# The first projection of an encoder trunk: loads three blocks ahead, c spread by matmuls, u made by ScalarE, VectorE's order skewed

## The chip, the cores and the metric

The kernel runs on one core of one Trainium2 chip. The metric is the device time of one execution in microseconds (us), the median of several runs. The engines are named as in the profile: PE is TensorE's matmul, PEld its weight load, DVE VectorE, ACT ScalarE, POOL GpSimd, SP the engine that here issues all transfers.

## The reference

Two layers of an encoder on a sequence of 512 frames with 1024 channels. Only the start of layer 0 matters here: the modulation by the conditioning vector c, and the projection of the modulated input.

```
c_act = silu(c)                                        # (1, 1024)
mods  = split(c_act @ w_ada[i] + b_ada[i], 6)          # shift, scale, gate, twice
sh1, sc1, g1, sh2, sc2, g2 = mods
u     = x * (1.0 + sc1) + sh1                          # (512, 1024)
# layer 0, mixer A (gated linear attention):
q, k, v, g, gk_lr = split(u @ w_in, ...)               # widths 512, 512, 1024, 1024, 16
log_a = log_sigmoid(gk_lr @ w_gk2 + b_gk) / 16
...                                                    # chunks of 64, then out projection
x     = layer_norm(alpha * x + (1.0 + g1) * y)         # then the squared-ReLU MLP
```

## The kernel before

Activations lie transposed, channels on the 128 partitions and frames along the row: x is eight tiles `xs[k]` of 128x512. A product of float32 accuracy is made of three matmuls on rounded parts: each operand is split into a rounded part (`hi`, type fp32r) and a rest (`lo`), and hi*hi, hi*lo and lo*hi are added up in PSUM. For a weight block, `whi` is a copy of `raw` by ACT and `wlo = raw - whi` a subtraction by DVE. For u, ACT makes `u[k][:, 0]` (the hi part, `ar` in the trace) as `xs[k] * scale + shift`; the value without rounding is `uf`, and `ar <- uf, ar` is the subtraction that gives the lo part.

The first projection makes q and k: 1024 output channels in eight PSUM banks `pss[0..7]`, each over all 512 frames. Its loop runs over eight blocks k of 128 input channels, because u for block k can be made as soon as the shift and the scale of these 128 channels are known. They come from two blocks of `w_ada`, stored transposed (`ada`, 128x1024): DVE multiplies such a block by `csil`, the silu of c spread over all partitions, and sums along the row (`SCALAR_TENSOR_TENSOR raw<-raw,csil`, accumulated into a column of `mods`). A small addition (`mods<-mods,col`) adds the bias. So block k needs two `ada` blocks (512 KB each), `xs[k]` (256 KB) and a weight block `w_qk[k]` (512 KB), and ends in 24 matmuls: eight hi*hi, eight hi*lo, eight lo*hi.

Each compute engine runs its instructions in the order in which they were written (class `InOrder`; this is why nearly every line of the profile is L47). SP issues the transfers in order too; a transfer waits at SP until the buffer that it writes is free. All `ada` and weight blocks share one pool of five buffers (`rawp`, tag "raw"), so that in the first projection a block takes three of the five. A second pool, `act`, has 26 buffers of 128x1024 for activations. The weight splits `whi` and `wlo` have four buffers each.

The list `plan` holds every weight and `ada` block in the order of use; `emit_unit` takes the next one, issues its transfer and writes its split. `fill` calls it until `state["look"]` blocks are ready. After the projection the eight banks are evacuated into `qk` (`af` in the trace), sixteen matmuls make the low-rank gate (`gk_w`), and two passes over `w_v` (`vpass`) follow, between whose blocks the gate is computed head by head (`prep`). The matmuls of `prep` need `gk_sb`, the evacuated gate.

Of the kernel before, what the change touches and what calls it, by code (L numbers as in the profile page):

```python
# [59 lines left out]
def trunk(ctx, tc, xT, c, ada, cols, gk1, gk2, w_qk, w_v, w_g, w_go, a_qk, a_v, a_tab,  # L60
# [22 lines left out]
    def act_r():  # L83
        return act.tile([P, 2, S], F32R, tag="act", name=nm("ar"))
# [4 lines left out]
    def tt(eng, o, a, b, op):  # L89
        eng.tensor_tensor(out=o, in0=a, in1=b, op=op)  # L90
# [4 lines left out]
    def lo_of(eng, o, x, hi):  # L95
        return eng.tensor_tensor(out=o, in0=x, in1=hi.bitcast(F32), op=ALU.subtract)
# [11 lines left out]
    nc.sync.dma_start(out=csil, in_=c.to_broadcast([P, D]))  # L108
# [3 lines left out]
    for _ in range(5):  # L112
        T.matmul(warm, one[:, 0:P], one, start=True, stop=True)
    A.activation(out=csil, in_=csil, func=AF.Silu)
# [12 lines left out]
    def ada_unit(l, t, k):  # L127
        raw = rawp.tile([P, D], F32, tag="raw", name=nm("raw"))
        nc.sync.dma_start(out=raw, in_=ada[l, t * 8 + k])
        if (l, t, k) == (0, SH1, 0):  # L130
            nc.sync.dma_start(out=col, in_=cols)
            for ll in range(2):
                for ty in (SC1, G1, SC2, G2):
                    b = C_ADA + ll * 48 + ty * 8
                    G.tensor_scalar(out=col[:, b:b + 8], in0=col[:, b:b + 8], scalar1=1.0, scalar2=None, op0=ALU.add)
            G.tensor_scalar(out=bq8, in0=col[:, C_BQ:C_BQ + 8], scalar1=0.125, scalar2=None, op0=ALU.mult)
            G.tensor_scalar(out=nbgk, in0=col[:, C_BGK:C_BGK + 4], scalar1=-1.0, scalar2=None, op0=ALU.mult)
            G.tensor_scalar(out=gn2, in0=col[:, C_GN:C_GN + 8], scalar1=-0.5, scalar2=None, op0=ALU.mult)
        if t == SC1 and l == 0:
            nc.sync.dma_start(out=xs[k], in_=xT[k * P:(k + 1) * P, :])  # L140
        i = t * 8 + k
        V.scalar_tensor_tensor(out=raw, in0=raw, scalar=1.0, in1=csil, op0=ALU.mult, op1=ALU.mult,
                               accum_out=mods[:, l, i:i + 1])
        if l == 0 and t in (SH1, SC1):
            if t == SC1:
                m2 = mods[:, 0, 0:16].rearrange("p (a b) -> p a b", b=8)[:, :, k:k + 1]
                c2 = col[:, C_ADA:C_ADA + 16].rearrange("p (a b) -> p a b", b=8)[:, :, k:k + 1]
                tt(V, m2, m2, c2, ALU.add)
        elif t == G2:
            tt(V, mods[:, l, i:i + 1], mods[:, l, i:i + 1], col[:, C_ADA + l * 48 + i:C_ADA + l * 48 + i + 1], ALU.add)  # L150
        elif k == KT - 1:
            m8 = mods[:, l, t * 8:t * 8 + 8]
            tt(V, m8, m8, col[:, C_ADA + l * 48 + t * 8:C_ADA + l * 48 + t * 8 + 8], ALU.add)

# [14 lines left out]
    def emit_unit():  # L169
# [23 lines left out]
        if state["pos"] == 3:  # L193
            for q in range(2):
                nc.sync.dma_start(out=raw[:, q * S:(q + 1) * S], in_=what[:, q * S:(q + 1) * S])
        else:
            nc.sync.dma_start(out=raw, in_=what)
        hi, lo = split_w(kind in "fF")
        if state["pos"] == 3:
            V.tensor_copy(hi[:, 0:S], raw[:, 0:S])  # L200
            later.append(lambda: A.copy(out=hi[:, S:D], in_=raw[:, S:D]))
            later.append(lambda: lo_of(V, lo, raw, hi))
            ready_w.append((hi, lo))
            return
        if kind == "s":
            for q in range(2):
                A.copy(out=hi[:, q * S:(q + 1) * S], in_=raw[:, q * S:(q + 1) * S])
        else:
            A.copy(out=hi, in_=raw)
# [48 lines left out]
    for k in range(KT):  # L258
        plan.append(("a", (0, SH1, k)))
        plan.append(("a", (0, SC1, k)))  # L260
        plan.append(("s", w_qk[k]))
# [360 lines left out]
    def gla():  # L622
# [9 lines left out]

        u = [act_r() for _ in range(KT)]
        pss = [bank() for _ in range(8)]
        gk_t = wp.tile([P, D], F32R, tag="whi", name="gk_w")
# [5 lines left out]
        G.memset(eps_rms, RMS_EPS)  # L641
        for k in range(KT):
            emit_unit()
            emit_unit()
            if k == 0:
                emit_unit()
            A.activation(out=u[k][:, 0, :], in_=xs[k], func=AF.Identity, scale=mod(0, SC1, k), bias=mod(0, SH1, k))
            uf = gt.tile([P, S], F32, tag="t1", name=nm("uf"))
            V.tensor_scalar(out=uf, in0=xs[k], scalar1=mod(0, SC1, k), scalar2=mod(0, SH1, k), op0=ALU.mult, op1=ALU.add)
            w = next_w()  # L650
            lo_of(V, u[k][:, 1, :], uf, u[k][:, 0, :])
            for m in range(8):
                T.matmul(pss[m], wk(w, m)[0], uk(u, k)[0], start=(k == 0), stop=False)
# [25 lines left out]
        state["look"] = 3  # L679
        qk = [act_f() for _ in range(4)]  # L680
        for h in range(4):
            A.activation(out=qk[h][:, 0, :], in_=pss[h], func=AF.Copy, scale=float(P) ** -0.5)
            A.copy(out=qk[h][:, 1, :], in_=pss[4 + h])
# [547 lines left out]
```

## Time and profile before

| | |
|---|---|
| median of 3 runs | 1232.88 us (1232.21 to 1233.76) |
| the profiled execution | 1231.73 us, its span 1229.5 us |
| PE busy | 1181.4 us (96%), 5834 matmuls |
| PEld busy | 986.9 us (80%) |
| DVE busy | 834.3 us (68%) |
| ACT busy | 542.9 us (44%) |
| POOL busy | 185.4 us (15%) |
| first projection, first weight load to the next stage's first | 10.96 to 61.34 us |

The busy shares are means over the whole span. Matmuls are pipelined, so that PE is counted as busy while one is still draining; the weight loads, one ahead of each matmul, show the pace better. The time outside the span (2.2 us) belongs to the start and the end of the execution.

### The profile page before, as it was taken

What the parts mean: (1) busy time and instruction counts of PE and PEld (TensorE: products, weight loads), DVE (VectorE), ACT (ScalarE), POOL (GpSimd) and SP (SyncE); (2) the same over time, 40 slices, a digit from 0 to 9 for tenths busy, and PEclk for the clock granted to TensorE, in tenths of its full rate; (3) what the DMA queues carried; (4) which work ended last, traced back from release to release, by engine and by line L of the source; (5) the groups of instructions that cost most, each with busy time, mean ns of one, the idle gap of its engine ahead of it and who ended that gap; (6) DMA issues with size and microseconds to landing.
All of it is one profiled execution on the core that took longest, in us unless ns stands there. A gap on an engine that the chain in (4) does not pass through costs nothing.

```text
span 1229.5 us, 15417 instructions
## 1 busy us (share of the span) xinstructions
PE 1181.4 (96%) x5834; PEld 986.9 (80%) x5834; DVE 834.3 (68%) x1269; ACT 542.9 (44%) x864; POOL 185.4 (15%) x195
## 2 busy tenths in 40 slices
PE   8999999899999999999999999898999999999995
PEld 5678887788888888888888877668888888888885
DVE  6779579787667676667864788889865443443467
ACT  3265566365243243343483565573642322322324
POOL 2000001620000000004631132226200000000035
PEclk9999999999999999999999999999999999999998
DMA  8846634118878888764025431322165332232201
GB/s 310 280 155 209 230 110 140 50 41 282 284 268 316 280 291 310 261 250 154 2 78 180 146 135 71 128 87 69 35 204 156 92 106 93 88 107 97 89 15 69
DMA packets 57274, 192.68 MB, mean 157 GB/s; under 512 B 6448, under 2 KB 10800, under 8 KB 57200
## 3 DMA queue, kind: packets, MB, share of 16 engines
q1 hardware_dynamic: 57200, 191.70, 45.7%
q8 instruction: 46, 0.75, 0.3%
q14 instruction: 28, 0.23, 0.1%
HBM read 172.80 MB, written 18.87 MB: 156 GB/s over the span
## 4 chain that ended last, share of the span: by engine, by line
PE 58%; DVE 20%; issue 9%; ACT 8%; POOL 3%; DMA 0%; ACTq 0%; DVEq 0%; POOLq 0%
PE ps L47 58%; DVE af L47 5%; ACT af L47 3%; DVE x L47 3%; DVE ar L47 3%; DVE raw L47 2%; DVE wlo L47 2%; ACT ar L47 2%; POOL af L47 1%; POOL x L47 1%; ACT whi L47 1%; DVE u L47 1%; DVE d L47 1%; DVE y L47 1%; ACT e L47 1%
## 5 line engine op out<-in xcount | busy, mean ns | idle before, releaser
L47 PE MATMUL ps<-ar,whi 128*128 128x512 f32 (+1 forms) x2816 | 806.0, 374 | 6.1 <-ACT ar L47 3.3
L47 PEld LDWEIGHTS ps<-ar,whi 128*128 128x128 f32 x2816 | 515.1, 190 | 104.8 <-DVE ar L47 5.3
L47 PE MATMUL ps<-ar,wlo 128*128 128x512 f32 (+1 forms) x1408 | 513.6, 371 | 0.2 <-DVE wlo L47 0.2
L47 PEld LDWEIGHTS ps<-ar,wlo 128*128 128x128 f32 x1408 | 267.0, 190 | 45.7 <-DVE wlo L47 0.8
L47 ACT CAST whi<-raw 128x1024 fp32r<-128x1024 f32 (+1 forms) x171 | 171.4, 1011 | 212.6 <-PE ps L47 187.0
L47 DVE TENSOR_TENSOR wlo<-raw,whi 128x1024 fp32r<-128x1024 f32 x160 | 199.9, 1254 | 33.3 <-ACT whi L47 31.2
L47 DVE SCALAR_TENSOR_TENSOR x<-ps,mods,x 128x512 f32<-128x512 f32 (+1 forms) x96 | 63.0, 658 | 126.4 <-PE ps L47 126.4
L47 POOL TENSOR_TENSOR x<-x,af 128x512 f32<-128x512 f32 x14 | 25.5, 1847 | 805.9 <-ACT af L47 805.9
L47 DVE SCALAR_TENSOR_TENSOR raw<-raw,csil 128x1024 f32<-128x1024 f32 x96 | 115.8, 1218 | 5.9 <-DMA raw<-ada 5.9
L47 DVE TENSOR_TENSOR h<-r 128x512 f32<-128x512 f32 (+1 forms) x72 | 49.2, 688 | 84.0 <-ACT r L47 83.1
L47 PE MATMUL ps<-ar,fhi 128*128 128x256 f32 (+1 forms) x448 | 91.9, 302 | 8.5 <-DVE ar L47 7.6
L47 ACT ACTIVATE r<-ps 128x512 f32<-128x512 f32 (+1 forms) x72 | 39.0, 548 | 130.7 <-PE ps L47 130.5
L47 PEld LDWEIGHTS ps<-ar,fhi 128*128 128x128 f32 x448 | 71.9, 191 | 12.6 <-DVE ar L47 9.0
L47 PE MATMUL ps<-whi,ar 128*128 128x512 f32 x256 | 81.0, 391 | 0.4 <-ACT whi L47 0.4
L47 DVE TENSOR_TENSOR ar<-h,ar 128x512 fp32r<-128x512 f32 (+1 forms) x72 | 45.5, 633 | 39.5 <-ACT ar L47 38.4
L47 PE MATMUL ps<-ar,flo 128*128 128x256 f32 (+1 forms) x224 | 66.9, 298 | 0.0
L47 ACT CAST ar<-h 128x512 fp32r<-128x512 f32 (+1 forms) x72 | 41.2, 573 | 51.8 <-DVE h L47 51.8
L47 PEld LDWEIGHTS ps<-whi,ar 128*128 128x128 f32 x256 | 48.1, 188 | 11.2 <-ACT whi L47 1.3
L47 PE MATMUL ps<-wlo,ar 128*128 128x512 f32 x128 | 50.2, 392 | 1.5 <-DVE wlo L47 1.5
L47 POOL PARTITION_ALL_REDUCE mb<-af x16 | 31.2, 1952 | 125.0 <-DVE af L47 106.7
L47 ACT ACTIVATE af<-x 128x256 f32<-128x256 f32 (+1 forms) x48 | 22.7, 486 | 57.4 <-POOL af L47 31.4
L47 PEld LDWEIGHTS ps<-ar,flo 128*128 128x128 f32 x224 | 42.8, 191 | 1.3
(144 smaller groups left out, 1072.3 us busy)
## 6 DMA issues: line engine op xcount, KB each, us to landing
raw<-f SPq DMA_DIRECT2D x128, 512.0 KB, 4.2
raw<-ada SPq DMA_DIRECT2D x96, 512.0 KB, 4.8
raw<-a_qk SPq DMA_DIRECT2D x16, 512.0 KB, 4.7
khi_q<-fhi SPq DMA_DIRECT2D x12, 512.0 KB, 3.0
klo_q<-flo SPq DMA_DIRECT2D x12, 512.0 KB, 4.4
wlo<-klo_q SPq DMA_DIRECT2D x12, 512.0 KB, 4.2
whi<-khi_q SPq DMA_DIRECT2D x12, 512.0 KB, 3.3
raw<-w_v SPq DMA_DIRECT2D x8, 512.0 KB, 4.5
```

The lines of the kernel that those rows point to most:

```text
L47: r = f(*a, **k)
```

## The change

- c is loaded as one row (`crow`, 4 KB) where it was loaded 128 times over (512 KB). Two matmuls with a row of ones spread it over the partitions into two PSUM banks (`cps`), and ACT takes the silu from there. They stand after the first of five matmuls on a tile of ones that were there before (`warm`).
- The transfers of block k (two `ada` blocks, `xs[k]`, `w_qk[k]`) are written three blocks ahead (`head_dma`). The `ada` blocks get buffers of the pool `act` (`hraw`) and no longer share the five `raw` buffers.
- ACT makes `uf`, in place of DVE.
- DVE's order is skewed: the multiplication for the shift of block k+1 stands ahead of the two subtractions of block k, that for its scale behind them (`head_ada`).
- The additions of 1 to the bias columns, eight POOL instructions, become one DVE instruction.
- The gate's padded weight `gk_w` moves from the pool of `whi` to `act`.
- After the projection, the split of the first `w_v` block is written ahead of the evacuation, the second in its middle, and DVE takes four of the eight evacuations from ACT.

```diff
-    nc.sync.dma_start(out=csil, in_=c.to_broadcast([P, D]))
+    crow = act.tile([P, D], F32, tag="act", name="crow")[0:1, :]
+    nc.sync.dma_start(out=crow, in_=c)
...
-    for _ in range(5):
+    T.matmul(warm, one[:, 0:P], one, start=True, stop=True)
+    for q in range(2):
+        cps = psp.tile([P, S], F32, tag="ps", name=f"cps{q}")
+        T.matmul(cps, one[0:1, 0:P], crow[:, q * S:(q + 1) * S], start=True, stop=True)
+        A.activation(out=csil[:, q * S:(q + 1) * S], in_=cps, func=AF.Silu)
+    for _ in range(4):
         T.matmul(warm, one[:, 0:P], one, start=True, stop=True)
-    A.activation(out=csil, in_=csil, func=AF.Silu)
...
+    def head_dma(k):
+        raws = []
+        for t in (SH1, SC1):
+            raws.append(act.tile([P, D], F32, tag="act", name=nm("hraw")))
+            nc.sync.dma_start(out=raws[-1], in_=ada[0, t * 8 + k])
+        if k == 0:
+            nc.sync.dma_start(out=col, in_=cols)
+        nc.sync.dma_start(out=xs[k], in_=xT[k * P:(k + 1) * P, :])
+        raw = rawp.tile([P, D], F32, tag="raw", name=nm("raw"))
...
+            nc.sync.dma_start(out=raw, in_=w_qk[k])
+        head[k] = raws + [raw]
+
+    def head_ada(k, t):
+        i = t * 8 + k
+        raw = head[k][t]
+        V.scalar_tensor_tensor(out=raw, in0=raw, scalar=1.0, in1=csil, op0=ALU.mult, op1=ALU.mult,
+                               accum_out=mods[:, 0, i:i + 1])
+        if t == SC1:
+            if k == 0:
+                c4 = col[:, C_ADA:C_ADA + 96].rearrange("p (a b c) -> p a b c", a=2, c=24)[:, :, :, 8:24]
+                V.tensor_scalar(out=c4, in0=c4, scalar1=1.0, scalar2=None, op0=ALU.add)
...
+            tt(V, m2, m2, c2, ALU.add)
...
+        for k in range(3):
+            head_dma(k)
...
+        head_ada(0, SH1)
+        head_ada(0, SC1)
         for k in range(KT):
-            emit_unit()
-            emit_unit()
+            if k + 3 < KT:
+                head_dma(k + 3)
...
+            if k:
+                w_half(0)
+                w_half(1)
+            else:
+                V.tensor_copy(w[0][:, 0:S], raw[:, 0:S])
+            A.activation(out=u[k][:, 0, :], in_=xs[k], func=AF.Identity, scale=mod(0, SC1, k), bias=mod(0, SH1, k))
+            A.activation(out=uf, in_=xs[k], func=AF.Identity, scale=mod(0, SC1, k), bias=mod(0, SH1, k))
             if k == 0:
-                emit_unit()
-            A.activation(out=u[k][:, 0, :], in_=xs[k], func=AF.Identity, scale=mod(0, SC1, k), bias=mod(0, SH1, k))
-            uf = gt.tile([P, S], F32, tag="t1", name=nm("uf"))
-            V.tensor_scalar(out=uf, in0=xs[k], scalar1=mod(0, SC1, k), scalar2=mod(0, SH1, k), op0=ALU.mult, op1=ALU.add)
-            w = next_w()
+                w_half(1)
...
+            if 0 < k < KT - 1:
+                head_ada(k + 1, SH1)
             lo_of(V, u[k][:, 1, :], uf, u[k][:, 0, :])
+            lo_of(V, w[1], raw, w[0])
+            if k == 0:
+                head_ada(1, SH1)
+            if k < KT - 1:
+                head_ada(k + 1, SC1)
...
         state["look"] = 3
+        fill(1)
         qk = [act_f() for _ in range(4)]
         for h in range(4):
             A.activation(out=qk[h][:, 0, :], in_=pss[h], func=AF.Copy, scale=float(P) ** -0.5)
-            A.copy(out=qk[h][:, 1, :], in_=pss[4 + h])
+            V.tensor_copy(qk[h][:, 1, :], pss[4 + h])
+            if h == 1:
+                fill(2)
         fill()
```

SP's transfers at the very start of the program, in the order in which they are issued. Before (`raw` of lines L129 are the `ada` blocks, two for block 0 and then two for block 1):

```order
L108 DMA csil<-c 128x1024
L129 DMA raw_139<-ada 128x1024
L131 DMA col<-cols 128x196
L129 DMA raw_154<-ada 128x1024
L140 DMA x_88<-xT 128x512
L195 DMA raw_159<-w_qk 128x512 x2
L129 DMA raw_195<-ada 128x1024
L129 DMA raw_198<-ada 128x1024
L140 DMA x_89<-xT 128x512
L197 DMA raw_206<-w_qk 128x1024
```

And of the change (`hraw` are the `ada` blocks):

```order
L109 DMA crow<-c 1x1024
L152 DMA col<-cols 128x196
L153 DMA x_94<-xT 128x512
L157 DMA raw_129<-w_qk 128x512 x2
L150 DMA hraw_123<-ada 128x1024
L150 DMA hraw_125<-ada 128x1024
L150 DMA hraw_132<-ada 128x1024
L150 DMA hraw_134<-ada 128x1024
L153 DMA x_95<-xT 128x512
L159 DMA raw_137<-w_qk 128x1024
```

Although `head_dma` writes the `ada` blocks first, x and the weights of block 0 now stand ahead of both `ada` blocks of block 0; the bytes up to and with the second `ada` block are 98 + 256 + 512 + 512 + 512 KB and the row of c, where they were 512 + 512 + 98 + 512 KB.

DVE's instructions around block 3, which stand for those of every block from 1 to 6. Before:

```order
L47 SCALAR_TENSOR_TENSOR raw_281,mods<-raw_281,csil 128x1024
L47 SCALAR_TENSOR_TENSOR raw_284,mods<-raw_284,csil 128x1024
L47 TENSOR_TENSOR mods<-mods,col 128x2
L47 TENSOR_SCALAR uf_290<-x_91,mods 128x512
L47 TENSOR_TENSOR wlo_295<-raw_292,whi_294 128x1024
L47 TENSOR_TENSOR ar_120<-uf_290,ar_120 128x512
```

And of the change:

```order
L47 SCALAR_TENSOR_TENSOR hraw_174,mods<-hraw_174,csil 128x1024
L47 TENSOR_TENSOR mods<-mods,col 128x2
L47 SCALAR_TENSOR_TENSOR hraw_218,mods<-hraw_218,csil 128x1024
L47 TENSOR_TENSOR ar_149<-uf_313,ar_149 128x512
L47 TENSOR_TENSOR wlo_312<-raw_177,whi_311 128x1024
L47 SCALAR_TENSOR_TENSOR hraw_220,mods<-hraw_220,csil 128x1024
L47 TENSOR_TENSOR mods<-mods,col 128x2
```

Before, the whole of block 3 (its `ada` sums, then its two subtractions) stands together. Now `hraw_218`, the first sum of block 4, stands between the bias addition of block 3 and its subtractions, and `hraw_220` behind them; `uf` is gone from DVE, and the lo part of u comes ahead of that of the weights.

DVE's instructions from the last subtraction of the projection on. Before:

```order
L47 TENSOR_TENSOR ar_137<-gk_sb,ar_137 112x512
L47 TENSOR_TENSOR wlo_533<-raw_530,whi_532 128x1024
L47 SCALAR_TENSOR_TENSOR raw_536,mods<-raw_536,csil 128x1024
L47 TENSOR_TENSOR wlo_542<-raw_539,whi_541 128x1024
L47 SCALAR_TENSOR_TENSOR raw_545,mods<-raw_545,csil 128x1024
L47 TENSOR_TENSOR wlo_551<-raw_548,whi_550 128x1024
L47 TENSOR_TENSOR gk_sb<-ps_554,gk_sb 48x512
L47 SCALAR_TENSOR_TENSOR raw_581,mods<-raw_581,csil 128x1024
L47 TENSOR_TENSOR wlo_587<-raw_584,whi_586 128x1024
L47 TENSOR_TENSOR L_621<-L_621,e_619 128x512
```

And of the change:

```order
L47 TENSOR_TENSOR wlo_520<-raw_517,whi_519 128x1024
L47 COPY af_523<-ps_158 128x512
L47 COPY af_524<-ps_159 128x512
L47 SCALAR_TENSOR_TENSOR raw_531,mods<-raw_531,csil 128x1024
L47 TENSOR_TENSOR wlo_537<-raw_534,whi_536 128x1024
L47 COPY af_525<-ps_160 128x512
L47 COPY af_526<-ps_161 128x512
L47 SCALAR_TENSOR_TENSOR raw_544,mods<-raw_544,csil 128x1024
L47 TENSOR_TENSOR wlo_550<-raw_547,whi_549 128x1024
L47 TENSOR_TENSOR gk_sb<-ps_553,gk_sb 48x512
L47 SCALAR_TENSOR_TENSOR raw_580,mods<-raw_580,csil 128x1024
L47 TENSOR_TENSOR wlo_586<-raw_583,whi_585 128x1024
```

Four evacuations (`af<-ps`) now stand between the splits; the first row, the lo part of the first `w_v` block, stands ahead of all evacuations on DVE, and the copy that makes its `whi` stands ahead of all evacuations on ACT. From `gk_sb` on the sequence is the old one, and on every engine the rest of the program keeps its order.

## Rows read from the trace of the kernel before

**Rows 1.** Windows: stretch, busy us (instructions) by engine, PE clock, DMA share, GB/s.
```profile
10.96:17.92 6.96, 6.96 (x24) 5.50 (x24) 5.27 (x8) 2.13 (x4) 2.90 (x8) 0.75 1.03 406
17.92:61.33 43.41, 41.48 (x169) 30.52 (x168) 31.81 (x54) 12.81 (x23) 0.00 (x0) 1.00 0.83 280
72.48:117.49 45.01, 44.35 (x214) 37.02 (x212) 40.00 (x60) 27.47 (x48) 0.00 (x0) 1.00 0.51 180
```
**Rows 2.** Windows, same columns: 100 us of the MLP.
```profile
300.00:400.00 100.00, 100.00 (x443) 82.81 (x442) 67.95 (x93) 35.38 (x42) 0.00 (x0) 1.00 0.83 292
```
**Rows 3.** Timeline of one block of the projection: start, us, engine, idle before.
```profile
36.31 1.69 PEld L47 LDWEIGHTS ps<-ar,whi 128*128 128x128 f32 x8 [0.34 <-ACT whi L47]
...
38.69 1.69 PEld L47 LDWEIGHTS ps<-ar,whi 128*128 128x128 f32 x8 [0.69 <-DVE ar L47]
...
41.16 0.82 ACT L47 ACTIVATE ar<-x,mods 128x512 fp32r<-128x512 f32 x1 [4.38 <-DVE mods L47]
...
42.54 0.53 PEld L47 LDWEIGHTS ps<-ar,whi 128*128 128x128 f32 x3 [0.35 <-ACT whi L47]
```
**Rows 4.** Waits of 17.92 to 61.33 us: total, times, longest.
```profile
PEld ps L47 <- DVE ar L47: 4.5, 7, 0.7
PEld ps L47 <- ACT whi L47: 2.5, 6, 0.8
```
**Rows 5.** Timeline of the start.
```profile
1.50 6.17 PE L47 MATMUL warm<-one 128*128 128x512 f32 x10 [1.50 <-DVE one L47]
...
2.65 0.43 SPq L140 DMA_DIRECT2D x<-xT  x1
...
5.11 1.06 ACT L47 ACTIVATE csil<-csil 128x1024 f32<-128x1024 f32 x1 [3.04 <-DMA csil<-c]
...
8.57 1.23 DVE L47 SCALAR_TENSOR_TENSOR raw<-raw,csil 128x1024 f32<-128x1024 f32 x1 [0.89 <-DMA raw<-ada]
...
10.96 0.50 PE L47 MATMUL ps<-ar,whi 128*128 128x512 f32 x1 [3.28 <-ACT ar L47]
...
13.78 2.28 PEld L47 LDWEIGHTS ps<-ar,whi 128*128 128x128 f32 x8 [0.28 <-DVE ar L47]
```
**Rows 6.** DMA issues, 2.6 to 2.8 us: count, size, us to landing.
```profile
x<-xT SPq DMA_DIRECT2D x1, 256.0 KB, 6.5
```
**Rows 7.** DMA issues of the whole span: two of c's size or shape.
```profile
csil<-c SPq DMA_DIRECT2D x1, 512.0 KB, 4.3
...
tab_c<-a_tab SPq DMA_DIRECT2D x1, 8.0 KB, 2.5
```
**Rows 8.** Windows, columns as in rows 1.
```profile
8.00:19.00 11.00, 8.04 (x28) 6.42 (x29) 8.34 (x14) 3.17 (x5) 5.86 (x16) 0.84 1.04 408
20.00:50.00 30.00, 28.58 (x117) 21.00 (x117) 22.99 (x42) 9.43 (x16) 0.00 (x0) 1.00 0.91 303
```
**Rows 9.** SP's own waits of 10 to 56 us: total, times, longest.
```profile
SPq L129 <- DVE wlo L47: 18.0, 7, 2.9
```
**Rows 10.** Timeline from the projection's end to the first gate.
```profile
65.58 1.23 DVE L47 TENSOR_TENSOR wlo<-raw,whi 128x1024 fp32r<-128x1024 f32 x1 [7.23 <-ACT whi L47]
65.60 0.19 PEld L47 LDWEIGHTS ps<-whi,ar 128*128 128x128 f32 x1 [0.67 <-ACT whi L47]
...
66.86 0.19 PEld L47 LDWEIGHTS ps<-wlo,ar 128*128 128x128 f32 x1 [1.07 <-DVE wlo L47]
...
72.13 0.30 PEld L47 LDWEIGHTS ps<-gk_sb,ar 112*128 112x128 f32 x2 [0.15 <-DVE gk_sb L47]
...
72.45 1.05 ACT L47 CAST whi<-raw 128x1024 fp32r<-128x1024 f32 x1 [4.58 <-DMA raw<-w_v]
...
76.92 0.69 DVE L47 TENSOR_TENSOR L<-L,e 128x512 f32<-128x512 f32 x1 [2.16 <-ACT e L47]
```
**Rows 11.** PE's waits of 62 to 117.6 us, the middle one of three.
```profile
PE ps L47 <- DVE at L47: 0.7, 1, 0.7
```
**Rows 12.** Groups by shape on DVE, 60 to 140 us: count, busy us, mean ns.
```profile
L47 DVE COPY af<-ps 128x512 f32<-128x512 f32 x4 | 2.6, 682 | 0.0
```

More of the change, by code (lines that the diff above doesn't have):

```diff
@@ L129, in ada_unit @@
         nc.sync.dma_start(out=raw, in_=ada[l, t * 8 + k])
[L130 to L140, printed above, removed]
         i = t * 8 + k
@@ L143, in ada_unit @@
                                accum_out=mods[:, l, i:i + 1])
[L144 to L149, printed above, removed]
+        if t == G2:
             tt(V, mods[:, l, i:i + 1], mods[:, l, i:i + 1], col[:, C_ADA + l * 48 + i:C_ADA + l * 48 + i + 1], ALU.add)
@@ L153, in ada_unit @@
             tt(V, m8, m8, col[:, C_ADA + l * 48 + t * 8:C_ADA + l * 48 + t * 8 + 8], ALU.add)
+    head = {}
+    def head_dma(k):
[8 more added lines that the diff above has]
+        if k == 0:
+            for q in range(2):
+                nc.sync.dma_start(out=raw[:, q * S:(q + 1) * S], in_=w_qk[k][:, q * S:(q + 1) * S])
+        else:
[10 more added lines that the diff above has]
+                V.tensor_scalar(out=c4, in0=c4, scalar1=1.0, scalar2=None, op0=ALU.add)
+            m2 = mods[:, 0, 0:16].rearrange("p (a b) -> p a b", b=8)[:, :, k:k + 1]
+            c2 = col[:, C_ADA:C_ADA + 16].rearrange("p (a b) -> p a b", b=8)[:, :, k:k + 1]
+            tt(V, m2, m2, c2, ALU.add)
     def mod(l, t, k):
@@ L192, in emit_unit @@
         raw = rawp.tile([P, D], F32, tag="raw", name=nm("raw"))
[L193 to L197, printed above, removed]
-        hi, lo = split_w(kind in "fF")
[L199 to L209, printed above, removed]
+        nc.sync.dma_start(out=raw, in_=what)
+        hi, lo = split_w(kind in "fF")
+        A.copy(out=hi, in_=raw)
         lo_of(G if kind in "pF" else V, lo, raw, hi)
@@ L256, in ada_list @@
         return [(l, t, k) for t in ts for k in range(8)]
[L258 to L261, printed above, removed]
     add_units([w_v[k] for k in range(8)], ada_list(0, G1))
@@ L631, in gla @@
         at = [gc.tile([P, S], F32, name=f"at{i}") for i in range(2)]
+        for k in range(3):
+            head_dma(k)
         u = [act_r() for _ in range(KT)]
         pss = [bank() for _ in range(8)]
-        gk_t = wp.tile([P, D], F32R, tag="whi", name="gk_w")
+        gk_t = act_r().rearrange("p a b -> p (a b)")
         gk_w = gk_t.rearrange("p (k c) -> p k c", c=P)
```

10 lines of the change are left out of this document (added).

## The prediction

> **What bounds the kernel now.** I first cut the span into the first projection and the stage behind it, by windows. Blocks 1 to 7 of the projection hold 168 weight loads in 43.41 us, 6.20 us for the 24 of a block, at a clock of 1.00 [rows 1]. In the MLP PE is never idle and loads 442 weights in 100 us, 0.226 us each [rows 2]; 24 at that pace are 5.43 us. So each of these blocks loses about 0.77 us, seven of them 5.4 us. DVE, busy 31.81 us of the 43.41, and the DMA engines, at 280 GB/s [rows 1], are not full. Where the time goes is seen in the timeline of one block [rows 3]: PE waits 0.34 us for `whi`, then 0.69 us for the lo part of u; ACT has stood idle 4.38 us until the bias addition `mods` let it make u, at 41.16, and the next block starts at 42.54, 6.23 us after the last. The waits add up to the same [rows 4]: 4.5 and 2.5 us, a part of which is covered by the matmul that still runs. It is a loop in order on DVE: both sums of a block, then `mods`, then across to ACT and back for the two subtractions, and only then the next block's sums.
>
> The start comes next [rows 5]. The silu of c is ready at 6.17 (5.11 + 1.06), but DVE's second sum starts at 8.57, when its `ada` block lands, and PE's first matmul 2.39 us later, at 10.96. Block 0 then takes 6.96 us at a mean clock of 0.75 [rows 1].
>
> Last the hand-over to the next stage [rows 10]: PE waits 0.67 us for the first `w_v` block's `whi`, 1.07 for its `wlo`, 0.15 for `gk_sb`. These splits are written behind the eight evacuations; DVE meanwhile stands idle for 7.23 us. Further on, between 72.48 and 117.49, DVE is busy 40.00 of 45.01 us [rows 1] and PE waits once, 0.7 us for DVE's `at` [rows 11].
>
> **The change, term by term.**
>
> *Blocks 1 to 7: -5.4 us.* DVE's work on a block was 31.81 / 7 = 4.54 us; without `uf` it is smaller. As a chain I count, with each instruction's length from a row: two sums of 1.23 [rows 5], a subtraction of 1.23 for the weights [rows 10], and half that for u, 0.6, and `mods` at most 0.2: 4.5 us, or 4.7 with a pause in which `hraw` of the next block ends before ACT's `uf` does. ACT was busy 12.81 / 7 = 1.83 us a block and gets one more instruction of at most 0.82, the length of its twin that makes the hi part [rows 3]: 2.65. Both are under 5.43, and the skew takes the trip to ACT out of DVE's loop, since DVE has the next block's sum to do in that time. So PE's own pace is the bound, and u and both splits are ready earlier by some 0.7 us with each block. If PE ran all blocks without a wait the saving is 43.4 - 38.0 = 5.4; from below I bound it by 4.6, if half the 0.34 us wait at each block's start and a little more stayed.
>
> *Supply.* A block is 1792 KB, 1.835 MB; at 5.43 us it needs 338 GB/s. From 8 to 19 us, with SP's queue full, the engines moved 408 GB/s, 4.5 us a block; from 20 to 50 us 303 [rows 8], but there SP stood waiting 18.0 us for DVE's `wlo` alone to free a buffer [rows 9]. With sixteen `hraw` in their own pool only the weight blocks share the five buffers, and the one of block 5 needs what block 0 has freed by 15 us. I cost supply at nothing. The other moves cost nothing either: POOL loses eight instructions, and those behind them that wait for the bias columns are first used in the gate, forty microseconds later; `gk_w` in `act` leaves all four `whi` buffers to the blocks.
>
> The Trainium skill, page "DMA: Bandwidth & Descriptors", section "Where 436 GB/s comes from", says that the HBM side binds such loads at about 358 GB/s a core; by that a block would take an estimated 5.13 us, still under PE's, and only the lead would shrink. The trace does not agree: 408 over 11 us is above it.
>
> *The start: +1.0 us at the end of block 0.* The order of SP's queue puts x and the weights ahead of both `ada` blocks. The bytes up to the second one, 1890 KB, are as many as before up to x, which was issued at 2.65 and landed 6.5 us later [rows 5, 6], at 9.15. The first large transfer was c's, the first; now it is the second or third, 0.4 to 0.9 us later in SP's queue at the 0.43 us that one issue takes [rows 5]. That gives 9.6 to 10.0; from the other side, if the first bytes flow no later and only those count, 8.57 as before. I take 9.6, which is 1.0 later than 8.57. DVE's new addition to the bias columns lies on the path too, 0.2 us, like `mods`. So PE starts at 10.96 + 1.2 = 12.2 (11.2 to 12.6). For block 0 I take the old 6.96 less its wait of 0.28 [rows 5], 6.7: it ends at 18.9, where it was 17.92. The wait goes because the lo part of u, now ahead of the weights' on DVE, is done some 1.5 us after PE starts, before eight slow matmuls are.
>
> Is c in time? A transfer of 8 KB landed after 2.5 us, c's old one of 512 KB after 4.3 [rows 7]; the single row lands by 3.3, at the latest 5.1. Seven matmuls of this kind now stand in the row; the old five took 6.17 us, 1.23 each [rows 5]. Two of them and half a silu, 0.6, put csil at 6.4, at the latest 8.2. The first `hraw` lands one 512 KB block before the second, at about 8.3 (1.3 us at 408 GB/s): c costs nothing in either case.
>
> Block 1 after that: DVE has its `mods` 0.9 us before PE's start, 11.3; then a copy, which ends while ACT makes `uf` (by 12.9), subtractions of 0.6 and 1.23, two sums and `mods`, 2.66: 17.4; ACT's u at 18.2. PE comes at 18.9. From here PE runs through, to 18.9 + 7 x 5.43 = 56.9, where it was 61.33: **-4.4** for the projection.
>
> *The hand-over: -1.8 us.* The first `w_v` block now needs nothing but a buffer that block 3 freed, and its split stands ahead of the evacuation: at 4.5 us a block it lands near 46, ten microseconds before it is used. Its two waits and the one for `gk_sb` go: 1.07 + 0.67 + 0.15, less about 0.1 of the ordinary gap. For `gk_sb` DVE needs, from the first free bank at about 56.2, four evacuations of 0.68 [rows 12], two sums and two subtractions of 1.23 and 0.7 for itself, 8.3 us: 64.5. PE asks for it after the gate's sixteen matmuls and the first 24 of `w_v`, 40 x 0.226 = 9.0, at 65.9. Covered by 1.4 us; were the cover gone, each microsecond is one on the path.
>
> *The stage behind: -0.7 us.* ACT waited 4.58 us for the fourth `w_v` block, and so `L`, the first step of a head's gate on DVE, came 4.8 us after the matmuls that it needs [rows 10]. SP issues that block when the first sum behind the evacuation is done, now at 58.8 or so; with the 4.3 us of c's it lands at 63.1, before those matmuls. DVE, after two more instructions, is free at 67.0; `L` comes about 3 us after the matmuls, since ACT has four steps of some 0.6 to do first. DVE's chain thus moves forward by 1.7 us more than PE, and the 0.7 us for `at` goes.
>
> Sum: -4.4 - 1.8 - 0.7 = -6.9 us. Against its own time the profiled run would be 1231.73 - 6.9 = 1224.8. It lay 1.15 below the median of the runs shown, so I forecast 1232.88 - 6.9 = **1226.0**.
>
> **The rivals.** *The start is not later (0.15).* The second `hraw` lands at 8.57, PE starts at 11.2, and the shorter pause behind seven warm matmuls keeps its clock at 2.4 GHz in block 0, where the pause was 3.28 us and the clock 0.75 of full [rows 1, 5]. Block 0 would end by 16.6; block 1's u, 1.0 earlier than above, at 17.2. Gain 1.7 more: 1224.3. Against it: the pause only shrinks by about a microsecond.
>
> *Given back in the stage behind (0.15).* DVE is 89% busy there and gets four evacuations, 2.7 us, in front of it. If it moves forward only with the projection, 4.4 us, PE meets it at `at` and the hand-over's gain turns into waits: 1228.5. For it speaks the share, against it the 7.23 us in which DVE stood idle at this very place.
>
> *The change doesn't do what it says (0.1).* The transfers run at the 303 GB/s of 20 to 50 us whatever the queue: 6.06 us a block. The last scale's block lands at 9.6 + 7 x 6.06 = 52.0, its weights 2.6 later, split by 56; PE ends near 61.2, as before, and keeps only the hand-over: about 1231.
>
> *Slower (0.05).* Supply falls further, as the transfers of three blocks share the engines and the one that is wanted next gets only its part. It decides from the point where a block takes over 6.4 us, 286 GB/s: then PE's end comes 2.5 us after the old one and eats the hand-over and `at` too. At 250 GB/s, 7.3 us a block, the last scale's block lands at 61.0, 9.0 later than in the case before: about 1239. The 408 GB/s with a full queue speak against it.
>
> **How the numbers follow.** The forecast has 0.55; its own range is 1224 to 1228, from a start between 11.2 and 12.6 and the bounds of 4.6 and 5.4 for the blocks. With the first two rivals it holds 0.85, so the range is 1223.0 to 1229.7. A measurement of this kernel can tell about 0.2%, 2.5 us, from no change: under 1230.4 lie the forecast and the first two rivals, 0.85; within it the third, 0.10; slower the last, 0.05.
>
> **What would show it.** In the projection of the changed kernel: weight loads of blocks 1 to 7 without a gap, 5.4 us a block; `hraw` landing ever further ahead of its sum; over 380 GB/s up to about 45 us. PE's first matmul between 11.2 and 12.6. No wait of PE at the first `w_v` block, none for `at`. The forecast is wrong if PE waits for u in late blocks (supply), if `hraw` of block 0 lands after 10.5, or if PE's waits turn up again, larger, before `at`.

## The result and the profile after

The changed kernel took 1225.16 us, the median of four runs (1224.23 to 1226.13); four runs of the kernel before beside them gave 1233.14. The ratio is 0.9936, 95% interval 0.9919 to 0.9953: 8.0 us less by the medians. The four runs lie in two pairs, near 1224.2 and 1226.1 us; what sets them apart was not traced. The profiled execution took 1224.23 us, 7.5 less than that of before, and its span is 7.0 us shorter (1229.5 and 1222.5); the forecast for it was 1224.8.

The page of the kernel after, its first lines:

```profile
span 1222.5 us, 15402 instructions
...
PE 1181.3 (97%) x5838; PEld 988.5 (81%) x5838; DVE 831.9 (68%) x1266; ACT 547.5 (45%) x869; POOL 181.8 (15%) x187
```

Windows of the kernel after: block 0, blocks 1 to 7, the stage behind; then the transfers of two stretches (columns as in [rows 1]):

```profile
13.09:19.00 5.91, 5.89 (x26) 4.36 (x25) 5.19 (x8) 3.18 (x6) 0.00 (x0) 1.00 1.03 410
19.00:56.99 37.99, 37.99 (x168) 31.46 (x168) 28.99 (x50) 19.14 (x31) 0.00 (x0) 1.00 0.86 320
72.48:117.49 45.01, 45.01 (x219) 37.84 (x217) 42.05 (x63) 27.52 (x49) 0.00 (x0) 1.00 0.52 180
...
8.00:19.00 11.00, 10.98 (x33) 6.18 (x31) 8.22 (x15) 5.26 (x8) 0.00 (x0) 1.00 1.03 409
20.00:50.00 30.00, 30.00 (x134) 24.82 (x133) 26.39 (x46) 17.02 (x27) 0.00 (x0) 1.00 0.94 357
```

The 168 weight loads of blocks 1 to 7 take 37.99 us where they took 43.41 [rows 1], 5.43 a block, and PE is busy for all of it: the pace of the MLP [rows 2]. Between 20 and 50 us the engines move 357 GB/s instead of 303 [rows 8]. Block 0 is a surprise: 5.91 us at a granted clock of 1.00, where it was 6.96 at 0.75.

The start of the kernel after, from its timeline:

```profile
3.50 0.50 PEld L47 LDWEIGHTS cps<-crow,one 1*128 1x128 f32 x2 [1.50 <-issue]
3.50 3.78 PE L47 MATMUL cps<-crow,one 1*128 1x512 f32 x4
...
7.21 0.50 PEld L47 LDWEIGHTS warm<-one 128*128 128x128 f32 x2 [1.50 <-issue]
...
7.32 0.60 ACT L47 ACTIVATE csil<-cps 128x512 f32<-128x512 f32 x1 [1.11 <-PE cps L47]
...
9.46 1.23 DVE L47 SCALAR_TENSOR_TENSOR hraw<-hraw,csil 128x1024 f32<-128x1024 f32 x1 [8.01 <-DMA hraw<-ada]
...
10.65 1.22 DVE L47 SCALAR_TENSOR_TENSOR hraw<-hraw,csil 128x1024 f32<-128x1024 f32 x1
...
12.23 0.81 ACT L47 ACTIVATE ar<-x,mods 128x512 fp32r<-128x512 f32 x1 [3.01 <-DVE mods L47]
...
13.09 0.76 PEld L47 LDWEIGHTS ps<-ar,whi 128*128 128x128 f32 x4 [0.73 <-ACT ar L47]
...
19.00 0.99 PEld L47 LDWEIGHTS ps<-ar,whi 128*128 128x128 f32 x5 [0.28 <-ACT ar L47]
```

PE's first matmul comes at 13.09, not 10.96 [rows 5]. The late piece is the first sum, not the second: `hraw` keeps DVE waiting until 9.46, and the second sum, at 10.65, waits for nothing. The silu of c is ready at 7.92 (7.32 + 0.60), later than before but still ahead of `hraw`. The weight loads of the matmuls on ones now last until 12.36, so that PE's weight loads pause for 0.73 us ahead of the projection. In the kernel before they paused for 4.11 (the 3.28 of [rows 5] is counted from the end of the last matmul, not of its weight load):

```profile
10.96 2.54 PEld L47 LDWEIGHTS ps<-ar,whi 128*128 128x128 f32 x8 [4.11 <-ACT ar L47]
```

The hand-over, from the same timeline:

```profile
56.74 1.29 DVE L47 COPY af<-ps 128x512 f32<-128x512 f32 x2 [4.93 <-PE ps L47]
...
56.99 3.59 PEld L47 LDWEIGHTS ps<-ar,ar 128*128 128x128 f32 x16
...
60.62 0.19 PEld L47 LDWEIGHTS ps<-whi,ar 128*128 128x128 f32 x1
...
60.85 0.19 PEld L47 LDWEIGHTS ps<-wlo,ar 128*128 128x128 f32 x1
...
63.81 0.69 DVE L47 TENSOR_TENSOR gk_sb<-ps,gk_sb 48x512 fp32r<-48x512 f32 x1
...
66.06 0.42 PEld L47 LDWEIGHTS ps<-gk_sb,ar 112*128 112x128 f32 x2
...
69.44 0.69 DVE L47 TENSOR_TENSOR L<-L,e 128x512 f32<-128x512 f32 x1 [2.54 <-ACT e L47]
```

No row of PE carries a wait: those for `whi`, `wlo` and `gk_sb` are gone [rows 10], and from 57 to 118 us the view of the waits has no row of PE at all, so the one for `at` [rows 11] is gone too.

Whether this lead reaches the end can be read at fixed points of the program. At each LayerNorm boundary ACT squares the mean of one half of the frames and then of the other (`d<-ps`; the third row of each view below is of the second half). These are the boundaries of the timelines, first the kernel before, then the kernel after:

```profile
231.67 0.38 ACT L47 ACTIVATE d<-ps 128x256 f32<-128x256 f32 x1 [2.12 <-PE ps L47]
...
591.81 0.38 ACT L47 ACTIVATE d<-ps 128x256 f32<-128x256 f32 x1 [1.60 <-PE ps L47]
...
863.96 0.36 ACT L47 ACTIVATE d<-ps 128x256 f32<-128x256 f32 x1
...
1205.64 0.38 ACT L47 ACTIVATE d<-ps 128x256 f32<-128x256 f32 x1 [1.83 <-PE ps L47]
```
```profile
224.86 0.38 ACT L47 ACTIVATE d<-ps 128x256 f32<-128x256 f32 x1 [2.19 <-PE ps L47]
...
584.99 0.38 ACT L47 ACTIVATE d<-ps 128x256 f32<-128x256 f32 x1 [1.60 <-PE ps L47]
...
856.91 0.36 ACT L47 ACTIVATE d<-ps 128x256 f32<-128x256 f32 x1
1198.62 0.39 ACT L47 ACTIVATE d<-ps 128x256 f32<-128x256 f32 x1 [1.86 <-PE ps L47]
```

The lead is 6.81, 6.82, 7.05 and 7.02 us, and 7.0 in the span: what is won by the first boundary stays won. Of the 6.81 the projection's end has 4.34 (61.33 to 56.99), and the hand-over with the stage behind 2.47.

### The profile page after: what moved, and what is told of

Same layout as the page of the kernel before. It is cut to its first block, busy times and chain, and to the rows that moved or that the text cites. A ratio compares the mean times of both kernels' runs of the same rounds, so it can differ in the third digit from the quotient of the medians.

```text
span 1222.5 us, 15402 instructions
## 1 busy us (share of the span) xinstructions
PE 1181.3 (97%) x5838; PEld 988.5 (81%) x5838; DVE 831.9 (68%) x1266; ACT 547.5 (45%) x869; POOL 181.8 (15%) x187
## 4 chain that ended last, share of the span: by engine, by line
PE 67%; DVE 15%; issue 9%; ACT 6%; POOL 3%; ACTq 0%; DVEq 0%; POOLq 0%
PE ps L47 66%; DVE af L47 5%; DVE x L47 3%; ACT af L47 2%; DVE ar L47 2%; POOL af L47 1%; ACT ar L47 1%; POOL x L47 1%; DVE u L47 1%; DVE wlo L47 1%; DVE d L47 1%; PE warm L47 1%; DVE y L47 1%; DVE t L47 0%; DVE raw L47 0%
## 5 line engine op out<-in xcount | busy, mean ns | idle before, releaser
L47 DVE SCALAR_TENSOR_TENSOR raw<-raw,csil 128x1024 f32<-128x1024 f32 x80 | 96.8, 1217 | 0.0
L47 ACT CAST ar<-h 128x512 fp32r<-128x512 f32 (+1 forms) x72 | 41.2, 572 | 51.9 <-DVE h L47 51.9
```

Of the source, the lines that this page charges most:

```text
L47: r = f(*a, **k)
```

## The experiments

Every kernel is the changed one with the edit shown. Runs of one group shared their runs of the kernel before, whose median lay between 1233.3 and 1233.6.

### Each half of the gain alone

**The evacuation and hand-over as before** (all eight banks on ACT, no split ahead of them):

```diff
-        fill(1)
         qk = [act_f() for _ in range(4)]
...
-            V.tensor_copy(qk[h][:, 1, :], pss[4 + h])
-            if h == 1:
-                fill(2)
+            A.copy(out=qk[h][:, 1, :], in_=pss[4 + h])
```

> The change, with only the hand-over put back: all eight evacuations on ACT, the first w_v split behind them. My theory (the hand-over was worth 1.8 us by itself and 0.7 us more in the stage behind): the projection ends at 57.0 us as in the changed kernel, PE again waits 0.6 to 0.7 us for the first w_v block's whi and about 1 us for its wlo, and the time is 1.8 to 2.5 us longer than the changed kernel's, near 1227.3. Rival (the stage behind is paced by DVE, so that what PE gains at the hand-over is given back there): the same two waits, but a time within 0.7 us of the changed kernel's, because a later wait shrinks by as much.

Measured: 1228.01 us (1227.37 to 1229.14). The projection ends at 56.88, as in the kernel after, and the old waits are back (view of PEld's waits, 17 to 118 us: total, times, longest):

```profile
PEld ps L47 <- DVE at L47: 1.3, 1, 1.3
PEld ps L47 <- DVE wlo L47: 1.1, 1, 1.1
PEld ps L47 <- ACT whi L47: 0.7, 1, 0.7
...
PEld ps L47 <- DVE gk_sb L47: 0.2, 1, 0.2
```

The first boundary comes at 227.61, 2.75 us after the changed kernel's. That is the hand-over's worth, `at` included (whose wait is 1.3 us here); the prediction's two terms add to 2.5.

**VectorE's order as before** (both sums of block k at its head, not skewed):

```diff
-        head_ada(0, SH1)
-        head_ada(0, SC1)
         for k in range(KT):
             if k + 3 < KT:
                 head_dma(k + 3)
+            head_ada(k, SH1)
+            head_ada(k, SC1)
...
-            if k == 0:
-                head_ada(1, SH1)
-            if k < KT - 1:
-                head_ada(k + 1, SC1)
```

> The change, with DVE's order unskewed: both sums of a block, its bias addition, then its two subtractions; transfers and buffers as in the change. My theory (the loop across DVE and ACT paced the blocks, the skew takes it out): DVE needs two sums 2.3, mods 0.3, then waits for ACT's u and uf 1.55, then 0.6 and 1.15, 5.9 us a block, so PE waits for u in every block from the second on, and the projection ends 2.5 to 3.5 us later than 57.0, at about 60; total near 1228. Rival (the transfers were late for want of buffers, and own buffers bring the gain): no wait, end at 57.0, time as the changed kernel's.

Measured: 1229.37 us (1227.61 to 1229.53). The projection ends at 60.58, 3.6 later; a block takes 5.9 us, and PE waits for u in each of them:

```profile
PEld ps L47 <- ACT ar L47: 4.1, 7, 1.0
...
19.38:60.58 41.20, 39.84 (x168) 31.00 (x168) 29.93 (x50) 18.90 (x31) 0.00 (x0) 1.00 0.76 278
```

(The second line is the window of its blocks 1 to 7.) This kernel has the transfers three blocks ahead, their own buffers and `uf` on ACT. With them its blocks 1 to 7 take 41.20 us instead of 43.41 and PE no longer waits for `whi`; as block 1 starts 1.46 us later than before the change, the projection ends only some 0.8 us earlier. The wait for u stays. The skew takes the blocks from 41.20 to 37.99 and is what makes PE run through.

### The rest of the change

**`uf` made by VectorE again:**

```diff
-            A.activation(out=uf, in_=xs[k], func=AF.Identity, scale=mod(0, SC1, k), bias=mod(0, SH1, k))
+            V.tensor_scalar(out=uf, in0=xs[k], scalar1=mod(0, SC1, k), scalar2=mod(0, SH1, k), op0=ALU.mult, op1=ALU.add)
```

> The change, with the unrounded u made by DVE again (one more DVE instruction of 0.55 us a block). My theory (DVE has 5.43 us for a block and needs 4.75, of which 0.45 is a wait for ACT's uf that then goes): 4.9 us a block, no wait of PE from block 2 on, end within 0.3 us of 57.0, time as the changed kernel's within 0.7 us. Rival (moving uf off DVE is a necessary part of the gain): about 0.5 us a block, end near 60, 3 us longer.

Measured: 1225.58 us (1224.72 to 1226.02). Blocks 1 to 7 lie between 18.55 and 56.63 us; DVE is busy 31.82 of these 38.08 us, and PE waits for nothing in them. In the skewed order DVE has room for `uf`; who makes it decides nothing.

**The `ada` blocks in the five shared buffers:**

```diff
-            raws.append(act.tile([P, D], F32, tag="act", name=nm("hraw")))
+            raws.append(rawp.tile([P, D], F32, tag="raw", name=nm("hraw")))
```

> The change, with the ada blocks back in the five shared raw buffers (which also puts block 0's ada blocks ahead of x and the weights in SP's queue). A scale's block can then only be issued when the weight block two blocks back is split, so a block takes at least issue to landing, 5 to 6 us. My theory (supply costs nothing in the change because of the own buffers): 5.6 to 6.1 us a block, PE waits for u again, end at 58 to 61, time 1 to 4 us longer than the changed kernel's. Rival (buffers are beside the point once DVE's order is skewed): 5.43 us a block, end at or before 57.0, since block 0's ada blocks come first: time as the changed kernel's or 0.5 us shorter.

Measured: 1225.10 us (1223.29 to 1226.38). What I expected did not come; the rival was right. With five buffers for everything a block still takes 5.42 us, and the engines move as much as with sixteen more buffers. Timeline and windows of this run:

```profile
7.95 1.23 DVE L47 SCALAR_TENSOR_TENSOR hraw<-hraw,csil 128x1024 f32<-128x1024 f32 x1 [6.50 <-ACT csil L47]
...
17.87 0.76 PEld L47 LDWEIGHTS ps<-ar,whi 128*128 128x128 f32 x4 [0.20 <-ACT ar L47]
```
```profile
20.00:50.00 30.00, 30.00 (x134) 24.83 (x133) 24.03 (x43) 16.15 (x26) 0.00 (x0) 1.00 0.97 358
```

SP's waits for `wlo` to free a buffer for the projection's blocks, 18.0 us in the kernel before [rows 9], are 7.8 us in this run between 10 and 56 us (4.6 and 3.2), with the same five buffers. So they followed in good part from DVE's late subtractions; with these on time five buffers do. Here SP's queue also has the first `ada` blocks ahead of x and the weights, the projection starts at 12.01, and it is csil that the first sum waits for.

**Own buffers, and only SP's queue in that other order:**

```diff
-            nc.sync.dma_start(out=raws[-1], in_=ada[0, t * 8 + k])
+            Y.dma_start(out=raws[-1], in_=ada[0, t * 8 + k])
...
-        nc.sync.dma_start(out=xs[k], in_=xT[k * P:(k + 1) * P, :])
+        Y.dma_start(out=xs[k], in_=xT[k * P:(k + 1) * P, :])
```

(`Y` is SP with its order as written, like the compute engines. In the trace c's row is still the first transfer; what has moved are the `ada` blocks of block 0, now ahead of x and the weights.)

> The changed kernel with its own buffers for the adaLN blocks, and only SyncE's queue in another order: the first six adaLN blocks and w_qk blocks ahead of c's row as in the run with shared buffers. Theory (the order of the queue alone sets when the projection starts, buffers nothing): first projection matmul at 12.0 us instead of 13.09, block 1 at 17.9, eight blocks of 5.44 without gaps, projection's end 55.9, and 1224 to 1225.3 us in all. Rival (the shared buffers did it): start stays at 13.1 and block 1 at 19.0, 1225.2.

Measured: 1225.31 us (1224.47 to 1226.44), first matmul at 11.97 and block 1 at 17.88. The order of the queue sets the start; the buffers had no part in it. The total did not follow: the profiled run of this kernel has the fall of the clock that the last group below is about, the kernel after's has not.

**The same order, and two of the four last matmuls on ones left out** (they compute nothing that is used):

> The change, with block 0's ada blocks ahead in SP's queue and two of the four last matmuls on ones left out (they compute nothing that is used). csil, at 7.9, then sets the start: first matmul at 12.0. My theory (in the change the clock was up at block 0 only because matmuls on ones ran until just before it): with a pause of one to two microseconds and two fewer matmuls the clock is at 1.2 GHz for part of block 0, which takes 6.5 to 7.5 us and ends at 18.5 to 19.5; time as the changed kernel's within 1 us. Rival (those matmuls do nothing for the clock): block 0 takes 5.9, ends at 17.9, time 1 us shorter.

Measured: 1223.31 us (1223.22 to 1226.08). The first matmul comes at 11.97 and block 0 takes 5.90 us: the rival was right. PE's weight loads at the projection's start:

```profile
11.97 0.76 PEld L47 LDWEIGHTS ps<-ar,whi 128*128 128x128 f32 x4 [2.55 <-ACT ar L47]
```

The last loads ahead of this pause took 0.34 us each, 0.85 us apart, those behind it 0.19: here the faster pace began in the pause.

**c spread by the transfer again**, with the five matmuls on ones of before:

```diff
-    nc.sync.dma_start(out=crow, in_=c)
+    nc.sync.dma_start(out=csil, in_=c.to_broadcast([P, D]))
```

> The change, with c again loaded 128 times over by one transfer and five matmuls on ones, no cps (SP's queue then has block 0's ada blocks ahead of x and the weights again). My theory (spreading c by matmuls made csil later, 7.9 us where it was 6.2, and the new SP order made the first ada block later still, 9.46; the start is a loss that the clock made good): PE's first matmul at 10.8 to 11.2, the clock falls in the pause as before the change, block 0 takes about 6.7 us and ends near 17.7 where the change has 19.0; projection ends near 55.7, time 1 to 1.5 us shorter than the changed kernel's. Rival (the 508 KB that the row saves bring block 0's ada blocks forward): first matmul 1.3 us later than the change's 13.1, time 1 us or more longer.

**The same with nine matmuls on ones:**

> The kernel with c loaded 128 times over, and nine matmuls on ones in place of five (four more that compute nothing that is used). My theory (clock and early start can both be had): first matmul at 10.8 to 11.2, clock at 2.4 GHz, block 0 5.5 to 6 us, ends by 16.9; projection ends near 54.9, time about 2 us shorter than the changed kernel's and 0.8 shorter than with five. Rival (the extra matmuls hold PE up or the clock falls all the same): block 0 ends at 17.7 or later, no gain over five.

Measured: 1224.45 us (1223.84 to 1224.83) and 1224.93 us (1224.35 to 1225.87). PEld's timelines at the projection's start, five and then nine matmuls:

```profile
10.40 0.76 PEld L47 LDWEIGHTS ps<-ar,whi 128*128 128x128 f32 x4 [3.54 <-ACT ar L47]
...
17.51 2.46 PEld L47 LDWEIGHTS ps<-ar,whi 128*128 128x128 f32 x11
```
```profile
10.61 0.19 PEld L47 LDWEIGHTS ps<-ar,whi 128*128 128x128 f32 x1 [0.24 <-issue]
...
16.85 3.29 PEld L47 LDWEIGHTS ps<-ar,whi 128*128 128x128 f32 x15 [0.59 <-ACT ar L47]
```

Here too SP's queue has the first `ada` blocks ahead of x, so the run to compare with is the one above that starts at 11.97: spreading c by matmuls costs the start 1.4 to 1.6 us, the order of the queue the other 1.1. With five matmuls PE's weight loads pause for 3.54 us, the granted clock falls 1.1 us into block 0 (0.50 from 11.6 to 15.2) and block 0 takes 7.11; with nine it takes 6.24 and the projection ends at 54.86, 2.1 us ahead of the kernel after. For this second run I expected a shorter total too, and that was wrong: it is the changed kernel's.

**Only the skew and the hand-over** (c by the transfer, shared buffers, `uf` on VectorE: the three edits above together):

> Of the change only DVE's skewed order and the hand-over (and the two moves that cost nothing, gk_w's pool and the bias addition on DVE): c loaded 128 times over, ada blocks in the five shared buffers, uf made by DVE. My theory (these two edits are the whole gain): 5.44 us a block from block 1 on, no waits at the hand-over, time as with c loaded 128 times over and all else of the change, within 0.7 us, so 0.5 to 2 us shorter than the changed kernel's. Rival (own buffers or ScalarE's uf matter once both are gone together): 5.6 us a block or more, projection end at 57 or later, time longer than the changed kernel's.

Measured: 1224.28 us (1223.84 to 1224.55). Window of its blocks 1 to 7:

```profile
16.73:54.74 38.01, 38.01 (x168) 31.45 (x168) 32.45 (x56) 14.11 (x24) 0.00 (x0) 1.00 0.95 338
```

The skew and the hand-over reach the whole gain without the other three. What the other three were worth without the skew is in the run with VectorE's old order, up to 2.2 us. In no run are the transfers written less than three blocks ahead, so that this part of the change was not tested by itself.

### Where an earlier start goes

The fixed points of the kernel with nine matmuls on ones (c by the transfer), in its timeline:

```profile
222.75 0.39 ACT L47 ACTIVATE d<-ps 128x256 f32<-128x256 f32 x1 [2.19 <-PE ps L47]
...
582.85 0.39 ACT L47 ACTIVATE d<-ps 128x256 f32<-128x256 f32 x1 [1.60 <-PE ps L47]
...
855.57 0.36 ACT L47 ACTIVATE d<-ps 128x256 f32<-128x256 f32 x1
...
1198.75 0.39 ACT L47 ACTIVATE d<-ps 128x256 f32<-128x256 f32 x1 [1.86 <-PE ps L47]
```

Its lead of 2.11 us over the kernel after is still 2.14 at 583 us, 1.34 at 856, and gone at 1199. Why 0.8 of it goes between 583 and 856 was not followed up. The clock of both falls at the boundaries, so I first blamed these and filled PE's pauses at the three inner ones with matmuls whose results nothing uses:

```diff
+            n_fill.append(0)
+            pre, mid = {1: (0, 8), 3: (0, 2), 5: (12, 0)}.get(len(n_fill), (0, 0))
+            for _ in range(pre):
+                T.matmul(dm[:, 0:P], ones_c, ones_c, start=True, stop=True)
             T.matmul(dm, ones_c, accz[:, hs], start=True, stop=not last)
+            for _ in range(mid):
+                T.matmul(qm, ones_c, accz[:, hs], start=True, stop=True)
```

In the changed kernel:

> The changed kernel, and in TensorE's pauses at the three inner LayerNorm boundaries (at 219 to 224, 582 to 585 and 837 to 841 us of its trace) 8, 2 and 12 matmuls that compute nothing that is used. Theory (TensorE's clock falls to half there because of the pauses; each fall was 3.41 us long and so costs up to 1.7 us of matmuls): with the pauses filled the granted clock stays at 1.00 through all three, up to 5.1 us less, 1220 to 1222 us. Rival (the falls come whatever TensorE does in the pauses, or the added matmuls make the real ones late): 1225 to 1227 us, with 0.66 to 0.85 of the clock at the boundaries.

In the kernel with nine matmuls on ones:

> The same fillers in the kernel with c by broadcast and nine matmuls on ones, whose projection ended 2.1 us earlier than the changed kernel's and whose total was the same. Theory (those 2.1 us were given back at the boundaries, by a longer fall at the first and an extra fall at 865 us): without the falls at the boundaries the lead stays, 1.5 to 2.5 us less than the changed kernel with filled pauses, 1218 to 1220 us; the fall at 865 us, whose pause is not filled, may stay and then costs 1.7 of it. Rival (the lead is lost elsewhere): the same time as the changed kernel with filled pauses, within 0.5 us.

Measured: 1225.19 us (1223.42 to 1225.79) and 1223.58 us (1223.43 to 1224.47). The clock did at these three places as expected, the time did not. The first boundary in the kernel after and with its pauses filled:

```profile
220.00:230.00 10.00, 6.40 (x39) 6.22 (x40) 4.82 (x11) 3.46 (x9) 6.33 (x10) 0.83 0.00 1
```
```profile
220.00:230.00 10.00, 9.65 (x65) 8.81 (x64) 4.82 (x11) 3.46 (x9) 6.85 (x10) 1.00 0.01 2
```

DVE and ACT do the same work in both, and from one half's statistics to the other's it is 16.09 us in the one (224.86 to 240.95) and 16.08 in the other: PE's slower matmuls there were covered. Ahead of the first statistics they were not: with the pauses filled the projection ended at 57.46, 0.47 us later than in the kernel after, and yet `d<-ps` came at the same 224.86. So this fall had cost about half a microsecond; my price of up to 1.7 us a fall was wrong. The two kernels themselves now stand 2.3 us apart in their spans (1224.1 and 1221.8), so a lead does last when both meet the same falls. What differs between runs is one more fall, behind a pause of 2.34 us that both kinds of run have at some 864 us; here it is in the kernel after and in the one with nine matmuls on ones:

```profile
866.10 0.39 PE L47 MATMUL ps<-ar,fhi 128*128 128x256 f32 x1 [2.34 <-DVE ar L47]
```
```profile
864.74 0.38 PE L47 MATMUL ps<-ar,fhi 128*128 128x256 f32 x1 [2.34 <-DVE ar L47]
```

Eight traces have a fall behind it (seven of them show 0.83 to 0.85 in 860 to 870, the run with VectorE's old order 0.69 in 870 to 875) and take 343.0 to 343.2 us from 856 to 1199. In five it stays at 1.00: the kernel after takes 341.71 (856.91 to 1198.62), the kernel before 341.68. So the last run shortens that pause too:

```diff
+        if len(n_fill) == 6:
+            for _ in range(9):
+                T.matmul(fb[0][:, 0:P], ones_c, ones_c, start=True, stop=True)
         fg(1, fb, range(8))
```

> The kernel with c by broadcast, nine matmuls on ones and the three LayerNorm pauses filled, and nine more unused matmuls ahead of the pause of 2.34 us at 861 to 864 us of its trace, after which its clock fell (0.70 in 865 to 870). Theory (that one fall is what lengthens the second MLP: from its first to its last LayerNorm statistics, 856 to 1199 us, the runs with a fall there took 343.0 to 343.2 us, those without one 341.7; and the falls at the other boundaries cost half a microsecond or less each): granted clock 1.00 in 860 to 870, that stretch 341.7 us, 1.4 us less than the run before it, 1222.0 to 1222.5 us, so 1.0 to 1.4 us below the changed kernel's lower runs and 2.5 to 3.2 below its median. Rival (the fall comes at another place, or the stretch is longer for another reason than the clock): 1223.5 us, stretch 343.2.

Measured: 1222.45 us (1221.82 to 1222.60, five runs; 0.9911 of before, 0.9898 to 0.9925). Windows of the kernel with three pauses filled, and of the one with four, with that one's fixed points:

```profile
860.00:870.00 10.00, 7.28 (x46) 6.88 (x45) 8.17 (x18) 7.71 (x15) 4.58 (x5) 0.83 0.01 2
```
```profile
860.00:870.00 10.00, 9.02 (x77) 8.82 (x76) 8.13 (x19) 7.72 (x15) 4.00 (x5) 1.00 0.01 2
```
```profile
855.27 0.36 ACT L47 ACTIVATE d<-ps 128x256 f32<-128x256 f32 x1
...
1196.98 0.38 ACT L47 ACTIVATE d<-ps 128x256 f32<-128x256 f32 x1 [1.83 <-PE ps L47]
```

The pause is down to 0.98 us and the stretch is 341.71 us. The kernel beats the changed one by 2.7 us in the medians and by 1.6 in the spans of the profiled executions (1222.5 and 1220.9), neither of which has the fall. In this trace the nine matmuls on ones kept the slow pace until 7.63 us, so that its projection began at 11.92, where the two other kernels with nine began at 10.61.

## Why the prediction was right, and where it was not

**Blocks 1 to 7, -5.4: right.** 43.41 to 37.99 us is -5.42, and the reason was the one given: the trip from DVE to ACT and back left the loop. With the skew there, a DVE relieved of `uf` and separate buffers, on which the prediction also counted, are not needed; without it the other edits bring 2.2 of the 5.4. The lower bound of 4.6 does not come out of its own words: half of 0.34 us in seven blocks is 1.2, which leaves 4.2.

**Supply at nothing: right.** 409 GB/s in 8 to 19 us and no wait of PE for a block. "Over 380 GB/s up to about 45 us" was not: 357 in 20 to 50. It was 404 to 406 GB/s up to 35 us; by 39.8 the last block's transfers were all issued, and after them SP stood 5.4 us for DVE's `wlo` again. The rival that saw the transfers stay at 303 mistook an effect of DVE's order for a limit.

**The start, +1.0 at the end of block 0: right in its sum (+1.08, 19.00 for 17.92), wrong in two terms that cancelled, which was luck.** "I take 9.6, which is 1.0 later" put the second `hraw` at 9.6; the second sum began at 10.65, held by the first, whose block landed at 9.46 instead of 8.3. The prediction had let the blocks land one after the other, 1.3 us apart at 408 GB/s. This is the window up to that landing:

```profile
0.00:9.46 9.46, 7.96 (x9) 2.83 (x10) 0.49 (x2) 3.76 (x4) 5.69 (x20) 1.00 0.64 219
```

The engines moved 219 GB/s on average (255 up to 8.57 us before the change), and not for that block alone: 219 GB/s over 9.46 us are 2.07 MB, while the transfers up to and with the first `ada` block are 1382 KB, 1.42 MB. By this estimate some 0.65 MB had gone to transfers that stood behind it. The first matmul at 13.09 lies outside 11.2 to 12.6. And "for block 0 I take the old 6.96 less its wait" assumed the clock of before; it stayed at 1.00, and block 0 took 5.91, not 6.7. Block 1 then still waited 0.28 us for u (row at 19.00), so that an even shorter block 0 would have gained nothing. The csil step was also short, 7.92 for 6.4: the two matmuls with one row took 3.78 us, where I had put 2 x 1.23. The 1.23 is a mean over a row of matmuls whose weight loads were 0.85 us apart until 4.94 and 0.43 after that; the two with one row stood at its slow beginning. It stayed within the 8.2 of its bound and cost nothing in this order of the queue. The rival "the start is not later" had the clock right and its cause half: the pause of the weight loads fell from 4.11 to 0.73 us, and not by a microsecond, because the matmuls on ones ran late.

**Projection's end 56.9: 56.99.**

**The hand-over and the stage behind, -2.5: right,** -2.47 at the first boundary and 2.75 when undone. `gk_sb` was done at 64.50, forecast 64.5, and asked for at 66.06, forecast 65.9; `L` came 7.48 us earlier and PE's `gk_sb` 6.07, so DVE moved forward by 1.4 more than PE, where 1.7 was forecast. Nothing was given back: DVE is busy 42.05 of 45.01 us and PE never waits for it.

**The total:** -6.9 forecast, -7.0 in the spans, -7.5 in the profiled executions' own times, -8.0 by the medians.

## What to carry to other kernels

Where engines run in order and a block's loop crosses from one engine to another and back, write the next block's independent work into the gap before adding buffers or moving operations: the skew took the blocks from 41.2 to 38.0 us, and with it in place buffers and `uf` gave nothing. Before a term for more buffers is believed, ask whether the transfers wait because buffers are few or because a late instruction holds them. And follow a lead at fixed points of the program to its end: of 2.1 us won at the start of this kernel some 1.5 vanished 860 us later with one fall of the clock, until a pause there was shortened.

## What was unexpected of the hardware

PE's weight loads stood for 1.50 us each time when the matmuls changed to weights of one row and back (3.50 and 7.21 us), where 0.52 was usual between slow ones. By its rows PE's matmuls ran on meanwhile (3.50 to 7.28 for the four passes with one row): from 3.50 to 7.21 are 3.71 us for four passes, 0.93 each, where 0.85 was the pace. So a change cost some 0.3 us, and most of the delay of csil is the slow pace. The loads of the matmuls on ones that came after were 0.85 us apart until 11.64. In other traces with the one-row matmuls the pace rose between 10.5 and 12.5 us or not ahead of the projection at all; without them it rose between 4.8 and 5.1, in one trace at 7.6. The clock columns show 1.00 through all of it, so at the very start the spacing is the better witness.

With the pause ahead of block 0 measured between weight loads, the granted clock was 1.00 all through block 0 behind pauses of 2.55 and 3.40 us, and fell to 0.50 in it behind 3.54 and 4.11. But a pause alone did not decide whether it fell: behind the same pause of 2.34 us between matmuls at some 864 us it fell in eight traces and not in five.
